# Mean shift of one quarter on VectorE, single PSUM tiles in four places, and one more weight block by seven products

## The chip, the cores and the metric

The kernel runs on one core of a Trainium2 chip. The metric is the device time of one execution in microseconds (us), lower is better. The engines are TensorE (PE in the profile, with its weight loads as PEld), VectorE (DVE), ScalarE (ACT), GpSimd (POOL) and SyncE (SP). SP and POOL issue most of the DMAs.

## The reference

A two-layer decoder trunk for one sequence of 256 tokens and 2048 channels, in float32. Layer 0 mixes tokens by causal pooling over windows of 2, 4, 8 and 16, layer 1 by causal attention with 16 heads of 128 channels, whose keys and values are computed once from the stream after layer 0. Each layer ends with a gated feed-forward network (FFN) that has a causal convolution of width 3.

```python
for i in range(DEPTH):                       # 2
    if i < N_A_LAYERS:                       # layer 0
        mix = pool_mixer(h, pool_w_in[i], pool_w_grp[i], pool_scale[i], pool_w_out[i])
    else:                                    # layer 1
        k_shared = (h @ shared_w_k).reshape(B_, S, N_HEADS, HEAD_DIM)
        v_shared = (h @ shared_w_v).reshape(B_, S, N_HEADS, HEAD_DIM)
        mix = dilated_attention(h, k_shared, v_shared, attn_w_q[j], attn_w_o[j])
    h = layer_norm(DEEPNORM_ALPHA * h + mix, ln1_g[i], ln1_b[i])
    ff = conv_ffn(h, ffn_w_up[i], ffn_conv_w[i], ffn_conv_b[i], ffn_w_down[i])
    h = layer_norm(DEEPNORM_ALPHA * h + ff, ln2_g[i], ln2_b[i])
```

The attention merges three branches of windows (128, 512, 2048) with strides 1, 4 and 16; the branches' softmax denominators weigh them.

## The kernel before

The stream is held transposed, with channels on the partitions, in four quarters of 512 channels: `H[q]` has 128 partitions, 4 channel blocks and 256 tokens. All weights together are read once. The work is a list of units. A unit is one block of weights, mostly 512 by 512 (1 MB): SP loads it to `raw`, ACT casts it to a high part `wh` (L99), DVE subtracts to get the low part `wl` (L100), and PE multiplies. A product in full precision is three: high by high, high by low, low by high (L180 and L181, or L183 to L185). Loads run five units ahead and splits three units ahead. `later(n, f)` puts `f` n units later, `before[i]` puts work ahead of the products of unit i; so each engine's order is fixed by the order in which this code is written out, SP's and POOL's DMA queues too.

For some blocks the 512 by 512 product is made by seven products of half the size in place of eight (Strassen-Winograd). Such a block takes two entries of the list, "a" and "b": DVE forms sums of the weights (L120 to L124), both engines split them (ACT L119 and L113, DVE L121 and L114), and PE does 42 products of 256 columns. Sums of the stream's quarter (`v_sums`, tile `f`, L1001 to L1021) are needed too, and the results are combined in `v_early` and `v_post`.

PSUM is handed out in four pairs of banks. `pair()` gives one pair, `bank()` the first half of one. An instruction that reads or writes a tile waits for the other engines' work on that tile as a whole.

The places of the change, in the order of the span:

- *Start.* `x_quad` (L538 on) transposes a quarter of x by PE (L548) into `xT`, two halves into the two banks of one pair. Per half, ACT casts to `xc` (L553) and DVE subtracts (L554). One unit later ACT copies all 1024 elements to `H` (L557).
- *Mean of the second layer norm of layer 0.* One unit after quarter 0 of the FFN's output is done, `shift` computes the negated partial mean `cs` by a product (L384) and ACT (L389). It is then added to the quarters: DVE for quarter 0 (L394), POOL's accumulate DMA for 1, 2 and 3 (L409). DVE adds the FFN's products (L338, L340) to each quarter, folds sums `S` and sums of squares `Q` (L364 to L370), and PE reduces them over partitions with L429 and L430. Between them the keys of head group 0 begin (tile `xp`).
- *Attention.* The heads are worked in four groups (`hq`) of four. For each group: units for k, q and v, then scores (PE L1064), softmax on DVE (L1067 to L1082) and ACT, a transposition on DVE (L1088, tile `pb`), sixteen small DMAs from SP and POOL to `pTs` (L1101), and the products with v (L1114, L1115, tile `o`), split by L1119 and L1120.
- *End.* `finish1` (L937 on) does the last layer norm for half of the tokens: PE forms bias terms in `gb` (L940, L947), DVE adds them (L952, L955).

Of the kernel before, what the change touches and what calls it, by code (L numbers as in the profile page):

```python
# [32 lines left out]
def trunk(ctx: ExitStack, tc: tile.TileContext, x, pool_w_in, pool_w_grp, pool_scale, pool_w_out,  # L33
# [348 lines left out]
    def shift(s, first, lay, which):  # L382
# [10 lines left out]
        def one():  # L393
            V.tensor_tensor(H[0], H[0], cb, OP.add)  # L394
            if first:
                pre(1)
            stats(0)

# [14 lines left out]
        if not first:  # L413
            for q in (1, 2, 3):
                less(q)
# [120 lines left out]
    def x_quad(q, halves=(0, 1)):  # L536
        xin = XIN
        if halves[0] == 0:  # L538
            H[q] = hp.tile([P, 4, T], F32, name="h", tag="h")
            XC[q] = quad_tile("xc")  # L540
        if halves[0] == 0:
            ST["xT"] = pair("xT")
        both = ST["xT"]
        for half in halves:
            for kk in range(2):
                for t in range(2):
                    k = 2 * half + kk
                    PE.transpose(both[:, half, kk * T + t * P:kk * T + t * P + P], xin[q, t][:, k * P:(k + 1) * P],  # L548
                                 ident)
        for half in halves:  # L550
            pv2 = both[:, half, :].rearrange("p (k t) -> p k t", k=2)
            s = slice(2 * half, 2 * half + 2)
            A.copy(XC[q][:, s, 0, :T], pv2)  # L553
            V.tensor_tensor(XC[q][:, s, 1, :T], pv2, XC[q][:, s, 0, :T].bitcast(F32), OP.subtract)  # L554
        if halves[-1] == 1:
            before.setdefault(min(q + 1, 3), []).append(
                lambda: A.copy(H[q], both.rearrange("p b (k t) -> p (b k) t", k=2)))  # L557

# [305 lines left out]
    def tm_post(lay, n, c):  # L864
# [68 lines left out]
        def finish1():  # L933
# [3 lines left out]
            g, b = [ST["g"][:, cc, :] for cc in range(4)], [ST["b"][:, cc, :] for cc in range(4)]  # L937
            ps = [p[:, i, :] for p in (pair("gb"), pair("gb")) for i in range(2)]
            for cc in range(3):
# [31 lines left out]
    def v_post(c):  # L971
        def post(t, ps):
            v = v_tile(c)[t]
            if c > 0:
                V.tensor_tensor(v, v, ps, OP.add)
            elif t == 0:
                A.copy(v, ps)
            else:
                V.tensor_copy(v, ps)
        return post  # L980
# [14 lines left out]
    def v_sums(q, then):  # L995
        ap = pools["attn"]
        x = H[q]
        a11, a12, a21, a22 = (x[:, k::2, t * P:t * P + P] for k, t in ((0, 0), (1, 0), (0, 1), (1, 1)))
        f = ap.tile([P, 4, T], F32, name="f", tag="k")
        d = [f[:, i].rearrange("p (k t) -> p k t", k=2) for i in range(4)]  # L1000
# [26 lines left out]
    def qk_post(nm, hq):  # L1027
# [3 lines left out]
        def evac(ps):  # L1031
# [11 lines left out]
            if nm == "q":  # L1043
# [7 lines left out]
                if hq == 0:  # L1051
                    later(4, lambda: v_sums(3, lambda: v_sums(1, lambda: v_sums(2, lambda: None))))
        return post
# [51 lines left out]
    def outputs(hq, ms):  # L1105
        if ms[0] == 0:
            oq[hq] = quad_tile("o")
        vt = vts[hq]
        both = pair("o")
        for m in ms:  # L1110
            hd = slice(m * P, (m + 1) * P)
            ps = both[:, m % 2, :]
            t = pT.pop((hq, m))
            PE.matmul(ps[:, :T], vt[:, 0, hd], t[:, :T], start=True, stop=False)  # L1114
            PE.matmul(ps[:, P:T], vt[:, 1, hd], t[:, T:], start=False, stop=True)  # L1115
        o = oq[hq][:, ms[0]:ms[0] + 2]
        for at in (slice(0, 1), slice(1, 2)) if hq == 3 else (slice(0, 2),):
            hi = o[:, at, 0, :T]
            A.copy(hi, both[:, at, :T])  # L1119
            V.tensor_tensor(o[:, at, 1, :T], both[:, at, :T], hi.bitcast(F32), OP.subtract)  # L1120

    def v_group(hq):
        js = (0, 1, 2, 3)
        seven = {0: (), 1: (1, 2, 3), 2: (1, 2, 3), 3: (3,)}[hq]
        group_tm(shared_w_v, rows4, 512 * hq, 512, xsrcs, v_post(hq),
# [152 lines left out]
```

## Time and profile before

| what | us |
|---|---|
| median of 3 runs | 2025.73 (2024.69 to 2026.8) |
| profiled execution, whole | 2024.98 |
| its span in the trace | 2023.2 |
| PE busy | 2011.6 (99%) |
| PE weight loads busy | 1813.7 (90%) |
| DVE busy | 1728.5 (85%) |
| ACT busy | 1269.2 (63%) |
| POOL busy | 94.3 (5%) |
| mean granted TensorE clock | 0.999 of full speed |

A row of the timeline gives the start in us, the duration, the engine, the line, the operation, what it writes and reads, and in brackets how long the engine stood idle before it and what ended that. The list of waits gives, for an engine, the idle time by the instruction that waited and what it waited for: total, times, mean. A row of windows gives the stretch, its length, the busy time of PE, PEld, DVE, ACT and POOL (with the number of instructions), then the granted clock, the DMA engines' busy share and GB/s.

### The profile page before, as it was taken

The numbers are of one execution on the slowest core, as the hardware profiler recorded it, in microseconds if no ns is written. First come the engines' busy times: TensorE is split into PE (matmuls) and PEld (weight loads), VectorE is DVE, ScalarE is ACT, GpSimd is POOL, SyncE is SP. The second block draws the span as 40 slices with busy tenths as digits, with TensorE's granted clock in tenths as the row PEclk, the third lists the DMA queues.
The fourth block names the chain that finished last, engine by engine and source line by source line (L and its number), as shares of the span: only waits on it lengthen the run. The fifth ranks groups of instructions, "written<-read, shape, count | busy, mean of one in ns | idle before, by whom it ended". The sixth has DMA issues, their size and how long they took to land.

```text
span 2023.2 us, 31428 instructions
## 1 busy us (share of the span) xinstructions
PE 2011.6 (99%) x12742; PEld 1813.7 (90%) x12742; DVE 1728.5 (85%) x1822; ACT 1269.2 (63%) x1546; POOL 94.3 (5%) x154
## 2 busy tenths in 40 slices
PE   9999999999999999999999999999999999999999
PEld 8898988999899988888898988998899989989987
DVE  6868887999899999779796878787899899989898
ACT  5454686766766676656554444477767677667672
POOL 2000000000000000000000021000000000000000
PEclk9999999999999999999999999999999999999999
DMA  8565576676666767885565656557666757666765
GB/s 256 192 211 188 164 216 191 180 221 222 197 198 205 233 190 219 236 226 187 177 207 165 199 175 207 188 175 221 167 215 203 227 179 227 193 222 189 211 220 173
DMA packets 271825, 408.30 MB, mean 202 GB/s; under 512 B 74446, under 2 KB 86116, under 8 KB 271424
## 3 DMA queue, kind: packets, MB, share of 16 engines
q1 hardware_dynamic: 259488, 388.93, 59.1%
q0 software_dynamic: 11760, 16.70, 5.5%
q8 instruction: 100, 1.64, 0.3%
q10 hardware_dynamic: 432, 0.66, 0.1%
q14 instruction: 45, 0.37, 0.1%
HBM read 380.01 MB, written 2.10 MB: 189 GB/s over the span
## 4 chain that ended last, share of the span: by engine, by line
PE 98%; DVE 1%; DMA 0%; issue 0%; ACT 0%; SPq 0%; DVEq 0%
PE acc L180 44%; PE acc L181 22%; PE s L246 3%; PE s L244 3%; PE s L245 3%; PE acc L185 3%; PE t L246 2%; PE t L244 2%; PE t L245 2%; PE acc L184 2%; PE acc L183 2%; PE t L255 2%; PE t L257 2%; PE t L256 2%; PE s L1064 0%; PE o L1114 0%
## 5 line engine op out<-in xcount | busy, mean ns | idle before, releaser
L180 PE MATMUL acc<-xc,wh 128*128 128x512 f32 x3264 | 1151.8, 396 | 0.0
L181 PE MATMUL acc<-xc,wl 128*128 128x256 f32 x3264 | 916.0, 281 | 0.0
L100 DVE TENSOR_TENSOR wl<-raw,wh 128x2048 fp32r<-128x2048 f32 (+2 forms) x305 | 657.1, 2163 | 174.9 <-ACT wh L99 170.3
L180 PEld LDWEIGHTS acc<-xc,wh 128*128 128x128 f32 x3264 | 616.0, 189 | 143.3
L99 ACT CAST wh<-raw 128x2048 fp32r<-128x2048 f32 (+2 forms) x305 | 548.7, 1805 | 170.1 <-PE acc L180 70.4
L181 PEld LDWEIGHTS acc<-xc,wl 128*128 128x128 f32 x3264 | 615.4, 189 | 0.1
L113 ACT CAST wh<-raw 128x1024 fp32r<-128x1024 f32 x142 | 148.4, 1052 | 194.5 <-DVE raw L122 175.3
L114 DVE TENSOR_TENSOR wl<-raw,wh 128x1024 fp32r<-128x1024 f32 x142 | 169.4, 1221 | 11.2 <-ACT wh L113 11.2
L121 DVE TENSOR_TENSOR wl<-raw,wh 128x1536 fp32r<-128x1536 f32 x71 | 124.5, 1754 | 6.7 <-ACT wh L119 5.7
L119 ACT CAST wh<-raw 128x1536 fp32r<-128x1536 f32 x71 | 104.9, 1477 | 35.4 <-PE acc L180 28.2
L287 POOL DMA_DIRECT2D ht<-w x48 | 41.3, 1014 | 1446.7 <-DVE ht L877 722.1
L246 PE MATMUL t<-wh,g 128*128 128x256 f32 x376 | 105.7, 281 | 0.0
L244 PE MATMUL t<-wh,g 128*128 128x256 f32 x376 | 105.6, 281 | 0.0
L245 PE MATMUL t<-wl,g 128*128 128x256 f32 x376 | 105.4, 280 | 0.0
L620 ACT ACTIVATE c<-u,cv 128x256 f32<-128x256 f32 x172 | 89.5, 592 | 23.1 <-DVE f L682 16.6
L246 PE MATMUL s<-wh,xs 128*128 128x256 f32 x344 | 96.2, 280 | 0.0
L244 PE MATMUL s<-wh,xs 128*128 128x256 f32 x344 | 96.1, 279 | 0.0
L245 PE MATMUL s<-wl,xs 128*128 128x256 f32 x344 | 96.0, 279 | 0.0
L124 DVE TENSOR_TENSOR raw<-raw 128x1024 f32<-128x1024 f32 x71 | 87.0, 1225 | 2.4
L625 ACT ACTIVATE a<-u,cv 128x256 f32<-128x256 f32 x172 | 73.4, 499 | 11.9 <-DVE g L692 11.9
L611 ACT COPY u<-acc 128x512 f32<-128x512 f32 x84 | 46.9, 573 | 47.4 <-PE acc L181 47.1
L625 ACT ACTIVATE u<-u,cv 128x256 f32<-128x256 f32 x172 | 73.4, 499 | 0.0
(337 smaller groups left out, 3445.2 us busy)
## 6 DMA issues: line engine op xcount, KB each, us to landing
raw<-in_ffn_w_up_dram SPq DMA_DIRECT2D x160, 1024.0 KB, 5.2
raw<-in_ffn_w_down_dram SPq DMA_DIRECT2D x80, 1024.0 KB, 5.2
raw<-in_pool_w_out_dram SPq DMA_DIRECT2D x16, 1024.0 KB, 5.0
raw<-in_shared_w_k_dram SPq DMA_DIRECT2D x16, 1024.0 KB, 5.1
raw<-in_attn_w_q_dram SPq DMA_DIRECT2D x16, 1024.0 KB, 5.1
raw<-in_shared_w_v_dram SPq DMA_DIRECT2D x16, 1024.0 KB, 5.2
raw<-in_attn_w_o_dram SPq DMA_DIRECT2D x16, 1024.0 KB, 5.4
ht<-w POOLq DMA_DIRECT2D x50, 256.0 KB, 5.3
```

What stands on the lines that cost most here:

```text
L99: A.copy(wh[i][:, s], r[:, s])
L100: V.tensor_tensor(wl[i][:, s], r[:, s], wh[i][:, s].bitcast(F32), OP.subtract)
L113: A.copy(h[:, :, n], r[:, :, n])
L114: V.tensor_tensor(l[:, :, n], r[:, :, n], h[:, :, n].bitcast(F32), OP.subtract)
L119: A.copy(hs, rs)
L121: V.tensor_tensor(ls, rs, hs.bitcast(F32), OP.subtract)
L180: PE.matmul(ps[m].ap, h[:, k, c], q[:, k, :, :T], start=st, stop=False)
L181: PE.matmul(ps[m][:, :T], l[:, k, c], q[:, k, 0, :T], start=False, stop=sp)
L244: PE.matmul(to, xh, h[:, k, n], start=opens and kk == 0, stop=False)
L245: PE.matmul(to, xh, l[:, k, n], start=False, stop=False)
L246: PE.matmul(to, xl, h[:, k, n], start=False, stop=ends and kk == 1)
L625: A.activation(to[:, m, :], u[:, m, i:i + T], AF.Copy, scale=cv[:, i, j:j + 1])
```

## The change

Five things are changed.

1. In the second layer norm of layer 0 DVE adds the mean to quarter 1 as well; POOL's accumulate DMA does so only for quarters 2 and 3.
2. In `x_quad` each half has its own PSUM tile. The copy to `H` is made in two parts of 512 elements, ahead of the products of unit q rather than q + 1.
3. In `finish1` the three products of `gb` have a tile each in place of two pairs.
4. In `outputs`, the second half of the last head group has one tile per head, and each is evacuated right behind its products. The first half of that group is evacuated by one instruction on each engine, as the other groups are.
5. Head group 0 does the block of quarter 3 of v by seven products. The sums of that quarter are formed as soon as q of group 0 is evacuated, in a buffer of the `h` pool; those of quarters 1 and 2 follow six units later. Since the list then has one more entry in this group, the second `blocks` and both `outputs` of the group come one block of weights sooner.

```diff
@@ shift, one
             V.tensor_tensor(H[0], H[0], cb, OP.add)
             if first:
                 pre(1)
+            else:
+                V.tensor_tensor(H[1], H[1], cb, OP.add)
             stats(0)
@@
         if not first:
-            for q in (1, 2, 3):
+            for q in (2, 3):
                 less(q)
@@ x_quad
-        if halves[0] == 0:
-            ST["xT"] = pair("xT")
-        both = ST["xT"]
         for half in halves:
+            ps = bank("xT")
             for kk in range(2):
                 for t in range(2):
                     k = 2 * half + kk
-                    PE.transpose(both[:, half, kk * T + t * P:kk * T + t * P + P], xin[q, t][:, k * P:(k + 1) * P],
-                                 ident)
-        for half in halves:
-            pv2 = both[:, half, :].rearrange("p (k t) -> p k t", k=2)
+                    PE.transpose(ps[:, kk * T + t * P:kk * T + t * P + P], xin[q, t][:, k * P:(k + 1) * P], ident)
+            pv2 = ps.rearrange("p (k t) -> p k t", k=2)
             s = slice(2 * half, 2 * half + 2)
             A.copy(XC[q][:, s, 0, :T], pv2)
             V.tensor_tensor(XC[q][:, s, 1, :T], pv2, XC[q][:, s, 0, :T].bitcast(F32), OP.subtract)
-        if halves[-1] == 1:
-            before.setdefault(min(q + 1, 3), []).append(
-                lambda: A.copy(H[q], both.rearrange("p b (k t) -> p (b k) t", k=2)))
+            before.setdefault(q, []).append(lambda s=s, pv2=pv2: A.copy(H[q][:, s, :], pv2))
@@ finish1
-            ps = [p[:, i, :] for p in (pair("gb"), pair("gb")) for i in range(2)]
+            ps = [bank("gb") for cc in range(3)]
@@ v_post
-            if c > 0:
-                V.tensor_tensor(v, v, ps, OP.add)
-            elif t == 0:
-                A.copy(v, ps)
-            else:
-                V.tensor_copy(v, ps)
+            V.tensor_tensor(v, v, ps, OP.add)
@@ v_sums
-        f = ap.tile([P, 4, T], F32, name="f", tag="k")
+        f = hp.tile([P, 4, T], F32, name="f", tag="h") if q == 3 else ap.tile([P, 4, T], F32, name="f", tag="k")
@@ qk_post
                 if hq == 0:
-                    later(4, lambda: v_sums(3, lambda: v_sums(1, lambda: v_sums(2, lambda: None))))
+                    v_sums(3, lambda: None)
+                    later(6, lambda: v_sums(1, lambda: v_sums(2, lambda: None)))
@@ outputs
-        both = pair("o")
+        last = hq == 3 and ms[0] == 2
+        both = None if last else pair("o")
         for m in ms:
             hd = slice(m * P, (m + 1) * P)
-            ps = both[:, m % 2, :]
+            ps = bank("o") if last else both[:, m % 2, :]
...
+            if last:
+                hi = oq[hq][:, m, 0, :T]
+                A.copy(hi, ps[:, :T])
+                V.tensor_tensor(oq[hq][:, m, 1, :T], ps[:, :T], hi.bitcast(F32), OP.subtract)
-        o = oq[hq][:, ms[0]:ms[0] + 2]
-        for at in (slice(0, 1), slice(1, 2)) if hq == 3 else (slice(0, 2),):
-            hi = o[:, at, 0, :T]
-            A.copy(hi, both[:, at, :T])
-            V.tensor_tensor(o[:, at, 1, :T], both[:, at, :T], hi.bitcast(F32), OP.subtract)
+        if not last:
+            o = oq[hq][:, ms[0]:ms[0] + 2]
+            A.copy(o[:, :, 0, :T], both[:, :, :T])
+            V.tensor_tensor(o[:, :, 1, :T], both[:, :, :T], o[:, :, 0, :T].bitcast(F32), OP.subtract)
@@ v_group
-        seven = {0: (), 1: (1, 2, 3), 2: (1, 2, 3), 3: (3,)}[hq]
+        seven = {0: (3,), 1: (1, 2, 3), 2: (1, 2, 3), 3: (3,)}[hq]
```

ScalarE's order at the start, before the change (`xT` are transposed halves, `raw` and `wh` the weights of the first units):

```order
7 L553 CAST xc<-xT 128x2x256 x2
8 L99 CAST wh_256<-raw_115 128x512 x4
9 L557 COPY h<-xT 128x1024
10 L553 CAST xc<-xT 128x2x256 x2
11 L99 CAST wh_332<-raw_124 128x512 x4
12 L557 COPY h<-xT 128x1024
```

And after it:

```order
7 L553 COPY h<-xT 128x512 x2
8 L551 CAST xc<-xT 128x2x256 x2
9 L99 CAST wh_260<-raw_115 128x512 x4
10 L553 COPY h<-xT 128x512 x2
11 L551 CAST xc<-xT 128x2x256 x2
12 L99 CAST wh_338<-raw_124 128x512 x4
```

The copy of a quarter is in two parts and now stands before the next quarter's casts even for the first quarter; the casts and the weights keep their order.

VectorE's order at the mean, before (`h` is a quarter of the stream, `cs` the negated mean, `fold` a scratch tile):

```order
655 L394 TENSOR_TENSOR h<-h,cs 128x1024
656 L364 TENSOR_TENSOR fold<-h 128x512
657 L367 TENSOR_TENSOR S<-fold 128x256
658 L364 TENSOR_TENSOR fold<-sq 128x512
659 L367 TENSOR_TENSOR Q<-fold 128x256
660 L338 TENSOR_TENSOR h<-h,acc 128x512
```

And after:

```order
655 L394 TENSOR_TENSOR h<-h,cs 128x1024
656 L398 TENSOR_TENSOR h<-h,cs 128x1024
657 L364 TENSOR_TENSOR fold<-h 128x512
658 L367 TENSOR_TENSOR S<-fold 128x256
659 L364 TENSOR_TENSOR fold<-sq 128x512
660 L367 TENSOR_TENSOR Q<-fold 128x256
661 L338 TENSOR_TENSOR h<-h,acc 128x512
```

One addition of 1024 elements stands ahead of the folds of quarter 0; the rest follows as before.

VectorE's order in the attention from q of head group 0 to its first scores (`p<-s`), before:

```order
724 L1042 TENSOR_TENSOR q<-q,acc 128x512 x2
725 L100 TENSOR_TENSOR wl_9294<-raw_9210,wh_9293 128x2048
726 L100 TENSOR_TENSOR wl_9325<-raw_9248,wh_9324 128x2048
727 L1067 SCALAR_TENSOR_TENSOR p<-s,negm 128x768
728 L1070 TENSOR_REDUCE mx<-p 128x2 x2
```

And after:

```order
725 L1033 TENSOR_TENSOR q<-q,acc 128x512 x2
726 L992 TENSOR_TENSOR f<-h 128x256
727 L993 TENSOR_TENSOR f<-f,h 128x256
728 L994 TENSOR_TENSOR f<-h 128x256
729 L995 TENSOR_TENSOR f<-h,f 128x256
730 L120 TENSOR_TENSOR raw_9218<-raw_9218 128x2x256
731 L121 TENSOR_TENSOR wl_9305<-raw_9218,wh_9304 128x2x768
732 L122 TENSOR_TENSOR raw_9218<-raw_9218 128x2x256
733 L124 TENSOR_TENSOR raw_9218<-raw_9218 128x4x256
734 L1012 TENSOR_TENSOR vs_9337<-f,vs_9337 128x256
735 L1012 TENSOR_TENSOR vs_9338<-f,vs_9338 128x256
736 L1012 TENSOR_TENSOR vsQ<-f,vsS 128x256
```

The sums of quarter 3 of the stream and the weight sums of the new seven-product block stand between q and the scores. The low part of that block's other half follows them and then the scores; of the two ordinary subtracts that stood here, the first was this block's own and is replaced by these steps, and the second comes after the scores' first softmax.

## The prediction

> **What bounds the kernel now.** I read the page first, then the list of what TensorE waits for, then the timeline at each of these places.
>
> ```profile
> span 2023.2 us, 31428 instructions
> PE 2011.6 (99%) x12742; PEld 1813.7 (90%) x12742; DVE 1728.5 (85%) x1822; ACT 1269.2 (63%) x1546; POOL 94.3 (5%) x154
> PE 98%; DVE 1%; DMA 0%; issue 0%; ACT 0%; SPq 0%; DVEq 0%
> ...
> PE acc L429 <- DVE S L370: 2.6, 1, 2.6
> ...
> PE acc L185 <- DVE wl L100: 0.9, 3, 0.3
> PE acc L430 <- DVE Q L370: 0.8, 1, 0.8
> ...
> PE acc L180 <- DVE o L1120: 0.5, 2, 0.2
> ```
>
> TensorE (PE) is busy for all but 11.6 us, so only three things can pay: a PE wait that goes, fewer PE columns, or a faster PE clock. The waits (us, times, mean) are small and each has a place. VectorE (DVE), busy 85%, is what PE waits for in every row shown; it can turn from helper into bound locally.
>
> The profiled execution took 2024.98 us, 1.78 more than its span and 0.75 under the median 2025.73. The sum below is made against 2024.98 and then put on the median by adding 0.75. From no change this kernel can be told only beyond about 0.2%, 4.05 us.
>
> **1. Mean shift of quarter 1 on VectorE.** Start, duration, engine, line; at the end the idle time and what ended it:
>
> ```profile
> 893.01 1.22 DVE L394 TENSOR_TENSOR h<-h,cs 128x1024 f32<-128x1024 f32 x1
> 896.32 0.43 DVE L367 TENSOR_TENSOR Q<-fold 128x256 f32<-128x256 f32 x1
> 901.48 0.69 DVE L338 TENSOR_TENSOR h<-h,acc 128x512 f32<-128x512 f32 x1 [4.73 <-DMA h<-cs]
> ...
> 930.28 1.28 DVE L338 TENSOR_TENSOR h<-h,acc 128x512 f32<-128x512 f32 x2
> 934.30 0.43 DVE L370 TENSOR_TENSOR Q<-Q,fold 128x256 f32<-128x256 f32 x1
> ...
> 924.73 0.28 PE L183 MATMUL acc<-xp,wh 128*128 128x258 f32 x1
> 930.38 0.28 PE L185 MATMUL acc<-xp,wl 128*128 128x258 f32 x1
> 933.27 0.70 PE L429 MATMUL acc<-S,onesd 128*128 128x256 f32 x2 [2.61 <-DVE S L370]
> 934.78 1.22 PE L430 MATMUL acc<-Q,onesd 128*128 128x256 f32 x2 [0.82 <-DVE Q L370]
> ...
> 904.96 1.49 ACT L99 CAST wh<-raw 128x1536 fp32r<-128x1536 f32 x1 [3.72 <-PE acc L180]
> 911.55 1.91 ACT L99 CAST wh<-raw 128x2048 fp32r<-128x2048 f32 x1 [4.05 <-DMA raw<-in_shared_w_k_dram]
> ```
>
> DVE idles 4.73 us for the accumulate DMA of quarter 1 and after 901.48 works without a gap until S and Q are done: that delay is what PE pays for 30 us later. The change puts one more instruction like the 1.22 us one ahead of the folds and drops one of three accumulate DMAs on POOL's queue; those of quarters 2 and 3 move up by one place and are needed 10 us later, so I cost them at nothing. The chain Q ends at 896.75 + 1.22 = 897.97, and L338 starts there and not at 901.48: 3.5 us sooner. I walked the row of DVE instructions on from there: each ScalarE input is there in time (the cast of 904.96 ends at 906.45 and its subtract would come at about 906.6; that of 911.55 ends at 913.46, needed at about 914.0), and the last quarter's products end about 924.9, needed at about 926.8. S is then ready at about 929.7, before PE gets there (930.5), and Q at about 931.2: of 2.61 + 0.82 = 3.43 us some 0.2 to 0.3 stay. Waits gained: 3.2.
>
> The wait has a second price, in the windows (busy PE, PEld, DVE, ACT, POOL, then granted clock):
>
> ```profile
> 934.00:934.80 0.80, 0.01 (x1) 0.02 (x1) 0.77 (x3) 0.80 (x1) 0.00 (x0) 1.00 0.95 366
> 934.80:935.40 0.60, 0.60 (x2) 0.51 (x3) 0.60 (x2) 0.60 (x1) 0.00 (x0) 0.50 0.04 14
> ...
> 938.00:938.40 0.40, 0.40 (x4) 0.40 (x4) 0.40 (x1) 0.00 (x0) 0.00 (x0) 0.74 0.00 0
> ```
>
> The granted clock is 0.50 from 934.8 to about 938.2, right after PE was idle for most of 930.5 to 934.6. Half speed for 3.4 us costs 1.7 us of work. If only 0.3 us of idle are left, I see no reason for the drop, and this is gained too. Together 3.2 + 1.7 = 4.9. Bounds: at most 3.43 + 1.7 = 5.1; at least −1.2, if the DMA's end was no true cause and the add is only one more 1.22 us on a busy engine. I take the upper part because every row between was walked.
>
> The Trainium skill, "TensorE: Matmul & The Clock Gate", Part 1, says that the clock gate falls to half rate after at least one idle window of about 3.4 us and rises again after such a window of work. The return after 3.4 us agrees; the fall differs, since here 2.61 us and 0.82 us with 0.7 us of products between them were enough. By the page's word alone the drop would not belong to this wait and the sum would be 1.7 lower, 6.1; the rows decide.
>
> **2. Two transposed tiles at the start.**
>
> ```profile
> 14.01 0.59 ACT L553 CAST xc<-xT 128x512 fp32r<-128x512 f32 x1 [0.76 <-DVE xc L554]
> 14.62 0.69 DVE L554 TENSOR_TENSOR xc<-xT,xc 128x512 fp32r<-128x512 f32 x1 [0.65 <-ACT xc L553]
> 15.97 0.39 PE L185 MATMUL acc<-xc,wl 128*128 128x256 f32 x1 [0.29 <-DVE wl L100]
> 16.57 1.01 ACT L557 COPY h<-xT 128x1024 f32<-128x1024 f32 x1
> 30.29 0.39 PE L185 MATMUL acc<-xc,wl 128*128 128x256 f32 x1 [0.35 <-DVE wl L100]
> 42.05 1.91 ACT L99 CAST wh<-raw 128x2048 fp32r<-128x2048 f32 x1 [4.70 <-DMA raw<-in_pool_w_in_dram]
> ```
>
> With both halves in one pair the two engines take turns: cast, subtract, cast, subtract. With a tile each, ScalarE goes on to the second cast while VectorE subtracts the first, and wl comes some 1.2 us sooner (0.76 less on ScalarE, 0.65 on VectorE), more than the waits it ends. The three waits sum to 0.9 in the list, and each product behind one is 0.11 longer than the 0.28 of a product that waits for nothing: 1.2. In the last quarter three more products run as late behind their subtracts (some 0.13 each by their spacing): 1.6, which I take, with 1.8 as the upper end and 0 as the other, since the load behind the cast at 42.05 was waited for 4.70 us and could swallow it. The copy to H goes from one of 1.01 to two of about 0.57 and moves up ahead of the next quarter's casts, where ScalarE idles over 2 us; the transposes now wait for it, done about 0.5 us sooner than they need it.
>
> **3. One tile per head for the last outputs.**
>
> ```profile
> 1235.66 0.50 PE L180 MATMUL acc<-o,wh 128*128 128x512 f32 x1 [0.23 <-DVE o L1120]
> 1236.52 0.50 PE L180 MATMUL acc<-o,wh 128*128 128x512 f32 x1 [0.24 <-DVE o L1120]
> ```
>
> The first head is evacuated while PE does the second's products, and the second's cast waits no more for the subtract. The two waits of 0.23 and 0.24, each with the 0.11 by which its product is longer than the 0.39 of an ordinary one, make 0.7, which I take; between 0 and 0.8. The other half of that head group, now evacuated in one piece, is needed a unit later and costs nothing.
>
> **4. Three tiles in the last layer norm.**
>
> ```profile
> 2015.57 2.84 PE L947 MATMUL gb<-g,dg 128*128 128x512 f32 x6
> 2017.59 1.41 DVE L952 SCALAR_TENSOR_TENSOR ht<-ht,mv,gb 128x512 f32<-128x512 f32 x2 [0.63 <-PE gb L947]
> ```
>
> DVE's first add waits for both products of a pair; with a tile each only for its own. Then the third product ends at 2018.41 and limits the last piece: 0.4 of 0.63, between 0 and 0.63.
>
> **5. Seven products for the last v unit, with its sums sooner.**
>
> ```profile
> L114 DVE TENSOR_TENSOR wl<-raw,wh 128x1024 fp32r<-128x1024 f32 x142 | 169.4, 1221 | 11.2 <-ACT wh L113 11.2
> L121 DVE TENSOR_TENSOR wl<-raw,wh 128x1536 fp32r<-128x1536 f32 x71 | 124.5, 1754 | 6.7 <-ACT wh L119 5.7
> ...
> 984.45 2.29 DVE L100 TENSOR_TENSOR wl<-raw,wh 128x2048 fp32r<-128x2048 f32 x1 [1.98 <-ACT wh L99]
> 989.37 0.96 DVE L1067 SCALAR_TENSOR_TENSOR p<-s,negm 128x768 f32<-128x768 f32 x1 [2.63 <-PE s L1064]
> 995.88 0.58 PE L255 MATMUL t<-wh,xc 128*128 128x512 f32 x1
> 1001.65 0.39 PE L180 MATMUL acc<-xc,wh 128*128 128x512 f32 x1
> 1042.21 4.60 DVE L100 TENSOR_TENSOR wl<-raw,wh 128x2048 fp32r<-128x2048 f32 x2
> 1047.29 0.39 PE L180 MATMUL acc<-xc,wh 128*128 128x512 f32 x1
> ...
> 989.00:1042.00 53.00, 53.00 (x308) 46.57 (x307) 50.51 (x81) 28.57 (x33) 9.11 (x16) 1.00 0.52 151
> ```
>
> An ordinary v unit takes PE 1001.65 − 995.88 = 5.77 us; 42 products of 256 columns at 0.12 us (5.65 us from 924.73 to 930.38, 47 steps) take 5.04. Gain 0.7, if nothing is late. DVE pays for it: 1.75 + 2 × 1.22, one more step of 1024 elements (1.22) and two of 512 (0.69 each, as L554) replace one 2.29: 4.5 more, some 0.2 less by the overlap of starts. The evacuation grows from one copy of 512 elements to two adds of 256 (0.43 each) and three of 512: about 2.1 more. Some 6.4 are added. The quarter's own sums (eight steps of 256 elements, about 3.2) only move, from after the scores to before them. The idle time before the scores takes 1.98 + 2.63 = 4.6. The rest, 1.8, and some 0.7 in which the second block's transposition waits for the transposed moves, go on as a debt of about 2.5, for from 989 to 1042 DVE is busy 50.51 of 53 us (the third number of the last row). Outputs come a unit sooner, and the eight SP moves now stand ahead of a weight load; the loads are five units ahead, which hides that. The debt reaches PE in the next head group's first q unit: its wl was done at 1044.5 and would be at 1047.0, with PE there at about 1046.5. So 0.5 of 0.7 is lost, net 0.2, between −1.5 (two more units late by half a microsecond or so and this one by 1) and 0.7.
>
> **Sum.** 4.9 + 1.6 + 0.7 + 0.4 + 0.2 = 7.8 us: 2024.98 − 7.8 = 2017.2, on the median 2017.9, 0.39% faster.
>
> **Rivals.**
> - *The wait is shortened, not removed.* If one step of my walk (a cast, a load of w_k) is late by 2 us, S comes after 930.5, about 1.7 us of waits stay, and the half clock with them. Part 1 then brings about 1.5, the total 4.4: 2021.3. For it: ScalarE waits 3.72 us for PE and 4.05 us for a load in this stretch; against: both end before DVE needs them.
> - *The mean does not pay.* The add itself delays the chain and another late input (the DMA of quarter 2, last matrix products) takes the removed wait's place. Parts 2 to 5 remain: 2.9, 2022.8, not to be told from before. Against: L338's products were done about 894.
> - *Slower: DVE's debt in the attention stage.* Place: 989 to 1047, where DVE has 2.5 us free in 53. If the 4.6 us of idle can't be used, because the raw weights or the scores come when they came before, the whole 6.4 us turns into PE waits; add the second transposition held by moves for up to about 5 us (POOL's busy 9.11 us in that window are two rounds of eight such moves, 4.6 each), and one more fall of the clock (1.7): 13.1 us. Then 2024.98 − 7.6 + 13.1 = 2030.5, on the median 2031.2. It decides from a loss of 11.7 us on, 7.6 + 4.05. Against: the seven products are used in later head groups with the same engines and the list shows no such wait there.
> - *The change does not do what it says* in the start: single tiles but the load at 42.05 sets the pace. That costs 1.6 and gives 2019.5, inside the first range.
> - *The clock falls anyway*, because another stretch of idle than that wait sets it off. Then 1.7 of part 1 stay lost: 6.1 gained, 2019.6. Against: over the span the clock averages 0.999, which this one fall of 1.7 in 2023 us already explains, and PE has no other wait over 1.1 us. I count it among the forecast's variants.
>
> **Chances.** Forecast, with its small variants, 0.70 (own range 2016.0 to 2020.0); shortened wait 0.14; mean without effect 0.10; slower 0.06. Faster by over 0.2% (under 2021.7): 0.70 and over half of the shortened wait, 0.79; within 0.2%: the rest of it and the mean without effect, less a little, 0.15; slower 0.06. The range begins at 2016.0, about all upper bounds (5.1 + 1.8 + 0.8 + 0.6 + 0.7 = 9.0, from 2025.73 2016.7) and some scatter, and ends at 2022.5, so that it takes in the shortened wait and leaves out half of the mean without effect and the slower case.
>
> **What would show it.** In the changed profile L429 should have no wait, L430 under 0.5, the granted clock 1.00 around 930 to 936, and L338 should follow Q without a DMA. The three waits at L185 and the two at L180 behind L1120 should be gone, L952's wait be about 0.2. A new wait of PE for wl, of about 0.5, should stand at the first q unit of the second head group. I am wrong if PE waits over 1 us anywhere after 985, or if the clock still falls near 932.

## The result

The changed kernel takes 2016.68 us (median of 6 runs, 2015.05 to 2018.46) against 2025.97 us for the kernel before in the same rounds (6 runs, 2024.69 to 2026.8). The ratio is 0.9955, with a 95% interval of 0.9942 to 0.9968. In later rounds, in the run called `e10_after_again` below, it was 0.9969 (0.9958 to 0.9981), 2016.49 us against 2022.69. So the change is worth 6 to 9 us; the forecast was 7.8. The changed kernel took the same time both times; it is the kernel before that differs, and the experiments show how it varies from one execution to the next.

First the list of what PE waits for in the changed kernel (us in total, times, longest; the third number of the lists ahead of the change is the longest wait too, not the mean, and no term of the prediction hangs on it):

```profile
PE acc L183 <- ACT wh L99: 1.6, 1, 1.6
PE warm L1159 <- DVE one L1155: 1.1, 1, 1.1
PE acc L181 <- DVE wl L100: 0.8, 1, 0.8
PE xT L548 <- DMA xin<-in_x_dram: 0.7, 1, 0.7
PE gb L943 <- DVE dg L941: 0.4, 1, 0.4
PE acc L185 <- DVE wl L100: 0.2, 1, 0.2
```

The waits for S and Q are gone, of the three at the start one of 0.2 is left, and the two behind the last outputs are gone. There are new ones: 1.6 us at the start for a cast, 0.8 us for `wl` and 0.4 us for `dg`. The 1.1 us for `one` at the very start are in both kernels.

The timeline at the mean, where L398 is the added instruction, and the windows behind it (the granted clock is the third number from the end):

```profile
891.14 1.22 DVE L394 TENSOR_TENSOR h<-h,cs 128x1024 f32<-128x1024 f32 x1
892.27 1.22 DVE L398 TENSOR_TENSOR h<-h,cs 128x1024 f32<-128x1024 f32 x1
895.80 0.68 DVE L338 TENSOR_TENSOR h<-h,acc 128x512 f32<-128x512 f32 x1
...
928.63 0.60 PE L431 MATMUL acc<-S,onesd 128*128 128x256 f32 x2
929.29 0.70 PE L432 MATMUL acc<-Q,onesd 128*128 128x256 f32 x2
```

```profile
928.00:932.00 4.00, 3.94 (x29) 3.49 (x28) 3.93 (x8) 3.79 (x5) 0.00 (x0) 1.00 0.35 134
932.00:936.00 4.00, 4.00 (x36) 4.00 (x35) 3.39 (x4) 2.30 (x2) 0.00 (x0) 1.00 0.41 113
```

L338 follows the folds with no wait, S is there when PE comes, and the clock stays at 1.00.

To see where the time went I took the start of each PE product in the changed trace less the start of the same product in the trace of before. A step in this offset is time won or lost at that place; a flat stretch is a stretch in which nothing changed. The same was done for the experiments, always against the first trace of before. The columns below are worked out in this way, in us:

| product of before, by its start | changed | e1 mean only | e2 no mean | e3 no seven | e4 kept busy |
|---|---|---|---|---|---|
| 12.38, behind the second transposes | +0.36 | +1.08 | +0.66 | +0.42 | +0.13 |
| 930.38, last before L429 | −1.87 | +1.20 | −1.61 | −1.79 | +0.13 |
| 938.17, behind the mean | −7.02 | −3.92 | −4.43 | −6.92 | −0.85 |
| 965 to 968, before the attention | −6.74 | −3.64 | −4.14 | −6.63 | −0.85 |
| 1052, second head group | −6.21 | −3.64 | −3.64 | −6.63 | −0.85 |
| 1236.52, behind the last outputs | −7.10 | −3.64 | −4.53 | −7.48 | −0.88 |
| 1990.6, last FFN | −8.22 | −3.64 | −5.65 | −7.48 | −0.88 |
| 2015.57, products with `dg` | −7.69 | −3.63 | −4.97 | −7.49 | −0.88 |
| end of the span | −8.3 | −3.7 | −5.5 | −8.2 | −0.9 |

For the changed kernel: the mean 5.1, the transposes 2.2 (from +0.36 to −1.87), the last outputs 0.89, and from `dg` to the end 0.6. The attention loses 0.5. Two more steps belong to no place that I had named: −1.1 spread over w_o and the second FFN, and +0.5 just ahead of `dg`.

### The profile page after: what moved, and what is told of

It reads as the page before. It is cut to its first block, busy times and chain, and to the rows that moved or that the text cites. A ratio compares the mean times of both kernels' runs of the same rounds, so it can differ in the third digit from the quotient of the medians.

```text
span 2014.9 us, 31474 instructions
## 1 busy us (share of the span) xinstructions
PE 2005.8 (100%) x12760; PEld 1810.2 (90%) x12760; DVE 1734.9 (86%) x1831; ACT 1269.7 (63%) x1551; POOL 93.0 (5%) x153
## 4 chain that ended last, share of the span: by engine, by line
PE 88%; DVE 7%; ACT 2%; DMA 2%; issue 1%; SPq 0%; DVEq 0%; ACTq 0%
PE acc L180 41%; PE acc L181 21%; PE s L244 3%; PE s L246 3%; PE s L245 3%; PE acc L184 2%; PE acc L185 2%; PE acc L183 2%; PE t L246 2%; PE t L244 2%; PE t L245 2%; DVE wl L100 2%; ACT wh L99 1%; DVE wl L114 1%; DVE wl L121 1%
## 5 line engine op out<-in xcount | busy, mean ns | idle before, releaser
L113 ACT CAST wh<-raw 128x1024 fp32r<-128x1024 f32 x144 | 150.7, 1052 | 202.8 <-DVE raw L122 175.5
```

Of the source, the lines that this page charges most:

```text
L113: A.copy(h[:, :, n], r[:, :, n])
```

## Experiments

### The mean alone, and all but the mean

`e1_mean_only` is the kernel before with this, and `e2_no_mean` the changed kernel without it:

```diff
             if first:
                 pre(1)
+            else:
+                V.tensor_tensor(H[1], H[1], cb, OP.add)
...
-            for q in (1, 2, 3):
+            for q in (2, 3):
```

> The kernel before with part 1 alone: VectorE adds the mean to quarter 1, the accumulate DMA does quarters 2 and 3. My theory (the wait of 2.61 + 0.82 us and the half clock behind it go together): about 5 us faster than before, some 2021, the trace the same as that of before up to about 928 and 5 us ahead of it from 932 on, granted clock 1.00 throughout. Rival (the parts need each other, as when the 3.5 us won on VectorE are used up elsewhere): the trace is less than 2 us ahead after 932, or loses part of it by 1050, and the time stays within 2 us of before.

> The changed kernel with part 1 undone (the DMA adds the mean to quarters 1, 2 and 3 again). My theory: 5 us slower than the changed kernel, about 2021.7, with waits of about 2.6 and 0.8 us at the reductions of S and Q and the granted clock at 0.50 for 3.4 us behind them. Rival (the sums of the mean came sooner through another part, the start for instance): under 2 us slower and no fall of the clock.

Measured: e1 2020.33 us, ratio to before 0.9981 (0.9972 to 0.9989), before 2024.7. Its trace makes the step of 5.1 us at the mean, like the changed kernel's, and keeps it through the attention: the theory holds and the parts don't need each other.

e2 2019.45 us, ratio 0.9973 (0.9964 to 0.9983). Neither expectation is met in full: without the mean on VectorE the step is 2.8 us and not 0, so undoing it costs 2.3 us in these two traces. The list of waits, the timeline and the windows of e2:

```profile
PE acc L429 <- DVE S L370: 1.3, 1, 1.3
...
PE acc L430 <- DVE Q L370: 0.8, 1, 0.8
```

```profile
898.58 0.69 DVE L338 TENSOR_TENSOR h<-h,acc 128x512 f32<-128x512 f32 x1 [3.44 <-DMA h<-cs]
```

```profile
932.00:936.00 4.00, 4.00 (x32) 3.95 (x33) 3.94 (x6) 2.40 (x4) 0.00 (x0) 1.00 0.00 2
936.00:940.00 4.00, 4.00 (x36) 4.00 (x35) 3.42 (x4) 2.28 (x2) 0.00 (x0) 1.00 0.83 256
```

VectorE's wait for the accumulate DMA is 3.44 us here and 4.73 in the trace of before, PE's wait for S 1.3 and not 2.6, and the clock does not fall. The DMA landed sooner: L338, which waits for it, starts 9.96 us after POOL's first issue (888.62), in the trace of before 11.25 us after it (890.23). What the mean on VectorE removes is thus a wait whose length differs from run to run.

### The kernel before once more

`e7_before_again` has no edit.

> The kernel before once more, for one look. Theory (the wait for S depends on when the accumulate DMA of quarter 1 lands, and this differs from run to run, 9.9 to 11.3 us after its issue so far; the clock falls only if the wait is long): with a landing near 9.9 us the wait for S is 1.2 to 1.4 us and the clock stays at 1.00, with one near 11.2 us it is 2.6 us and the clock falls to 0.50. Rival (the landing is the same in every run of this kernel): landing 11.2 us, wait 2.6 us, clock 0.50 again.

Measured, in one profiled execution: 2026.5 us. The waits, the timeline and the window:

```profile
PE acc L429 <- DVE S L370: 2.9, 1, 2.9
...
PE acc L430 <- DVE Q L370: 0.8, 1, 0.8
```

```profile
902.95 0.69 DVE L338 TENSOR_TENSOR h<-h,acc 128x512 f32<-128x512 f32 x1 [5.01 <-DMA h<-cs]
```

```profile
936.00:940.00 4.00, 3.76 (x17) 3.58 (x17) 4.00 (x7) 2.84 (x3) 0.00 (x0) 0.57 0.06 22
```

L338 starts 11.53 us after the issue, the wait is 2.9, the clock falls. So of three traces in which PE waits behind this DMA, the two in which L338 starts over 11 us after the issue have the long wait and the fall, and the one with 9.96 has neither. That fits the theory of e7, though a trace of the kernel before itself, unedited and with an early landing, is missing.

It also fits the spread: the kernel before ran between 2021.2 and 2028.0 us over all rounds of these experiments, e1 between 2019.7 and 2021.4. The mean granted clock of every execution is on record as well. Of 78 executions of the kernel before, 24 have a mean of 1.000 and took 2021.2 to 2023.6 us, 39 have 0.999 (2021.7 to 2026.3) and 15 have 0.998 or less (2024.8 to 2028.0); one stretch of 3.41 us at half clock is 0.0008 of such a mean. So in about a third of its executions the kernel before runs without any fall, and it is quicker then. The means do not tell whether a fall lay at the mean shift or at the start, where e7 has one too.

### Work in the wait

`e4_keep` is the kernel before with products that keep PE busy in the wait and that nobody reads:

```diff
+    KEEP = 20
...
     def chain(ps, lay, which, after):
+        if lay == 0 and which == 1:
+            keep = bank("keep")
+            for i in range(KEEP):
+                PE.matmul(keep[:, :P], ident, ident, start=True, stop=True)
```

> The kernel before with 20 products of 128 columns that nobody reads, in the wait ahead of the reductions of S and Q after the first FFN (about 2 us of work in a wait of 2.6). It takes away the idle time and not the wait. My theory (the clock falls because PE is idle there): S and Q come as late as before, the granted clock stays 1.00, and the trace is 1.7 us ahead of before from 940 on: about 2024. Rival (the clock falls for another reason, or the 1.7 us are not a loss): the clock still falls to 0.50 near 934, and the time is that of before.

Measured: 2024.48 us, ratio 1.0003 (0.9994 to 1.0012). The expected time of 2024 is met and says nothing, since before ran at 2024.7 there. The trace tells more:

```profile
930.64 4.63 PE L433 MATMUL keep<-ident 128*128 128x128 f32 x40
935.10 0.60 PE L434 MATMUL acc<-S,onesd 128*128 128x256 f32 x2
935.54 0.59 PE L435 MATMUL acc<-Q,onesd 128*128 128x256 f32 x2
```

```profile
932.00:936.00 4.00, 4.00 (x35) 3.90 (x34) 3.93 (x9) 2.61 (x4) 0.00 (x0) 1.00 0.47 180
936.00:940.00 4.00, 4.00 (x35) 4.00 (x34) 3.33 (x3) 3.80 (x4) 0.00 (x0) 1.00 0.31 86
```

The products took 4.6 us and not 2, so the reduction of Q starts later than before: at 935.54, and 0.63 later when the +0.13 of the start is taken off. Yet the products behind it are 0.98 ahead (from +0.13 to −0.85). The clock stayed at 1.00, and that is worth 0.98 + 0.63 = 1.6 us. So my 1.7 stands as the price of the fall.

That PE's idleness brought the fall is not shown by this run, for S and Q did not come as late as in the trace of before. The DMA landed early here, 10.0 us after its issue at 890.37:

```profile
900.37 0.69 DVE L339 TENSOR_TENSOR h<-h,acc 128x512 f32<-128x512 f32 x1 [3.50 <-DMA h<-cs]
```

S was ready at 932.1, so without the added products PE would have waited about 1.3 us for it, and with that wait the clock of e2 did not fall either.

What speaks for idleness is the record of the clock itself. In all 14 traces the times between two changes of the granted clock are whole multiples of 3.413 us: in the trace of before it is 271 of them from the rise at 9.78 to the fall at 934.79, and one from there to the next rise. So the changes lie on a grid that does not start with the wait. The two windows of the grid around the fall, in the trace of before:

```profile
931.38:934.78 3.40, 0.70 (x2) 0.30 (x2) 3.23 (x8) 3.40 (x8) 0.00 (x0) 1.00 0.92 308
934.80:938.20 3.40, 3.40 (x14) 3.22 (x15) 3.40 (x5) 2.59 (x3) 0.00 (x0) 0.50 0.01 2
```

PE was busy for 0.70 us of the window that ended with the fall, and for 0.70 us of that in e7 too. In e2 the two windows over the wait hold 2.01 and 2.69 us of work. Where the grid lies differs from run to run, so whether a wait of 2.6 us always brings the fall is not shown.

### Without the seven products

`e3_no_seven` is the changed kernel with part 5 undone:

```diff
-            V.tensor_tensor(v, v, ps, OP.add)
+            if c > 0:
+                V.tensor_tensor(v, v, ps, OP.add)
+            elif t == 0:
+                A.copy(v, ps)
+            else:
+                V.tensor_copy(v, ps)
...
-        f = hp.tile([P, 4, T], F32, name="f", tag="h") if q == 3 else ap.tile([P, 4, T], F32, name="f", tag="k")
+        f = ap.tile([P, 4, T], F32, name="f", tag="k")
...
-                    v_sums(3, lambda: None)
-                    later(6, lambda: v_sums(1, lambda: v_sums(2, lambda: None)))
+                    later(4, lambda: v_sums(3, lambda: v_sums(1, lambda: v_sums(2, lambda: None))))
...
-        seven = {0: (3,), 1: (1, 2, 3), 2: (1, 2, 3), 3: (3,)}[hq]
+        seven = {0: (), 1: (1, 2, 3), 2: (1, 2, 3), 3: (3,)}[hq]
```

> The changed kernel with part 5 undone (the first head group's last v unit in the ordinary way, its sums where they were). If part 5 pays 0.2 us as predicted, this is 0.2 us slower than the changed kernel. Rival, from the new wait of 0.84 us of the matrix products for wl at 1041: part 5 costs 0.3 to 0.8 us, and this kernel is that much faster than the changed one; the trace then has no wait of PE between 940 and 1060 and stays about 7 us ahead of before through that stretch.

Measured: 2016.84 us, ratio 0.9962 (0.995 to 0.9975), not to be told from the changed kernel. In the stretch itself the rival is right. The offsets of the changed kernel go from −6.74 to −7.41 at 1037, so the shorter unit gains the 0.7 us that I counted; then the wait comes, and the offset is −6.21 behind it. Here e3 stays at −6.63 with no wait. The rows of the changed kernel:

```profile
1039.95 0.40 PE L180 MATMUL acc<-xc,wh 128*128 128x512 f32 x1
1041.19 0.38 PE L181 MATMUL acc<-xc,wl 128*128 128x256 f32 x1 [0.84 <-DVE wl L100]
...
1034.76 2.23 ACT L113 CAST wh<-raw 128x1024 fp32r<-128x1024 f32 x2 [3.10 <-DVE raw L122]
1036.90 3.71 ACT L99 CAST wh<-raw 128x2048 fp32r<-128x2048 f32 x2
...
1038.84 4.49 DVE L100 TENSOR_TENSOR wl<-raw,wh 128x2048 fp32r<-128x2048 f32 x2 [0.59 <-ACT wh L99]
```

The stall is 1.1 to 1.2 us in all, as the offsets show. The block's `wl` is done at about 1041.1. In before it was done at 1044.5, which less the lead of 6.74 with which the attention began is 1037.8: the debt is 3.3 us. ScalarE is no help, since it waits 3.10 us for VectorE's weight sums (L122) before it comes to this block's cast.

The trace of e3 shows which item of the debt I had wrong. From the evacuation of q of head group 0 to the start of this block's `wl`, VectorE is busy 62.53 us in the changed kernel and 56.42 in e3: 6.1 more, about the 6.4 that I had added up. But of the 4.6 us of idle time ahead of the scores that I set against them, counted in the trace of before, e3 has only 1.55 + 1.85 = 3.4:

```profile
978.60 2.29 DVE L100 TENSOR_TENSOR wl<-raw,wh 128x2048 fp32r<-128x2048 f32 x1 [1.55 <-ACT wh L99]
982.75 0.96 DVE L1063 SCALAR_TENSOR_TENSOR p<-s,negm 128x768 f32<-128x768 f32 x1 [1.85 <-PE s L1060]
```

The other parts had used up the rest: in the changed kernel PE comes to the attention 6.7 us ahead of before and VectorE to q of this group only 5.5 (973.49 for 978.98), so VectorE has 1.2 us less to wait. With the 0.59 us for which it now waits for ScalarE at this block, 6.1 − 3.4 + 0.59 gives the 3.3; directly against e3 this `wl` starts 3.0 us later (1038.84 for 1035.86).

What makes the times equal lies elsewhere. In w_o and the second FFN the changed kernel gains 1.1 us on before, e2 does the same, and e3 and e1 nothing. There is no wait in it. From the start of a product of 512 columns to that of the next product it takes 233.3 to 233.5 ns on the mean in before, e1 and e3, and 232.7 to 232.8 in the changed kernel and e2 (some 1300 such steps that the traces show one by one between 1330 and 1960): 0.6 to 0.8 us of the 1.1, the rest is spread over other products. It repeats to the nanosecond: over that stretch the offset moves by −0.897 us in each of the five traces with part 5 (e5, e6 and e10 below among them) and by 0.000 in the eight others. At the end half of it is lost again, since VectorE is busy from 1992 on with one gap of 0.36 us, and `dg` comes when VectorE gets there (PE's wait of 0.4).

### VectorE's sums on GpSimd

If the new wait is VectorE's debt, taking work off VectorE should end it. `e5_pool_sums` is the changed kernel with the sums of quarters 1 and 2 on GpSimd; `e6_pool_both` moves three multiplications ahead of the last layer norm too:

```diff
+        E = V if q == 3 else nc.gpsimd
-        V.tensor_tensor(d[0], a21, a22, OP.add)
+        E.tensor_tensor(d[0], a21, a22, OP.add)
...
-                    V.tensor_tensor(z, z, ST["g"][:, cc, :], OP.mult)
+                    (nc.gpsimd if t else V).tensor_tensor(z, z, ST["g"][:, cc, :], OP.mult)
```

> The changed kernel, with the sums of quarters 1 and 2 for the first head group (eight steps of 256 elements, about 3 us of VectorE) moved to GpSimd. Theory (the wait for wl at 1041 is VectorE's debt from the seven products): the debt shrinks by 3 us, the wait of 0.84 us goes, and the trace is about 1 us further ahead of the changed kernel from 1045 on; at the end VectorE limits, so the time falls by 0.3 to 0.8 us. Rival (the wait comes from ScalarE's cast or the load of w_q, not from VectorE): the wait stays at about 0.8 us and the time is that of the changed kernel.

> As the run before, and the three multiplications of the second half of the tokens by the gain, ahead of the last layer norm (1.85 us of VectorE), on GpSimd too. Theory (over the last 15 us VectorE has no free time and sets the end): the products for the bias terms wait no more for dg (0.39 us in the changed kernel) and the end comes 0.5 to 1 us sooner than in the run before. Rival (the end is set by the last products, or GpSimd slows VectorE): no gain or a loss against the run before.

Measured: e5 2019.24 us, ratio 0.9976 (0.9967 to 0.9986); e6 2019.0, ratio 0.9978 (0.9969 to 0.9987): both slower than the changed kernel, and neither theory nor rival had foreseen it for e5. The rows of e5, on GpSimd and VectorE, and its new waits of PE:

```profile
1007.56 2.54 POOL L993 TENSOR_TENSOR f<-h 128x256 f32<-128x256 f32 x1
1010.17 2.67 POOL L994 TENSOR_TENSOR f<-f,h 128x256 f32<-128x256 f32 x1
1012.81 0.73 POOL L995 TENSOR_TENSOR f<-h 128x256 f32<-128x256 f32 x1
...
1015.34 1.23 DVE L305 TENSOR_TENSOR xsum<-f,xsum 128x1024 fp32r<-128x1024 f32 x1 [2.20 <-ACT xsum L309]
```

```profile
PE o L1108 <- DVE k L1034: 1.5, 1, 1.5
...
PE acc L181 <- DVE wl L100: 0.8, 1, 0.8
PE s L245 <- DVE wl L114: 0.5, 1, 0.5
```

A step that takes VectorE 0.42 us takes GpSimd 0.73 to 2.67. VectorE's next step on the sums stands in its queue and waits for them, through ScalarE's cast of them (L309), 2.20 and 1.11 us, so VectorE has won nothing; the wait for `wl` is as long as before, and through the attention this trace loses 2.9 us (−4.94 to −2.05) where the changed one loses 0.5. Whether a smaller debt would end the wait stays open, since the experiment did not make it smaller.

VectorE is slowed as well. The subtraction ahead of the end, in the changed kernel and, with GpSimd multiplying beside it, in e6:

```profile
1990.28 1.75 DVE L100 TENSOR_TENSOR wl<-raw,wh 128x1536 fp32r<-128x1536 f32 x1
```

```profile
1993.65 2.78 DVE L100 TENSOR_TENSOR wl<-raw,wh 128x1536 fp32r<-128x1536 f32 x1
```

The Trainium skill, "SBUF — State Buffer", "SBUF: two separate sides", says that VectorE with two inputs from SBUF and GpSimd share a port and that one blocks the other for a whole instruction. That VectorE is slower beside GpSimd agrees with the 2.78 for 1.75 us; that it is blocked for a whole instruction these rows do not show. The end still came a little sooner in e6 than in e5: PE's wait for `dg` is 0.2 and not 0.5, and from 1990 on e6 gains 0.3 us, less than the 0.5 to 1 us that I expected (the other 0.2 us between the spans, 2018.7 and 2019.2, are there from the start). Even this is not shown to come from GpSimd, for the changed kernel without an edit has a wait of 0.2 us for `dg` in `e10_after_again` below.

### What makes the second FFN quicker

Part 5 shifts three rings of buffers by one place: the PSUM pairs, the weight buffers and the h buffers. Four runs were meant to put e3 into the changed kernel's places, one ring at a time (`e8_pad`, `e9_shift`, `e12_hshift`) and two together (`e11_pad_shift`):

```diff
@@ e8_pad and e11_pad_shift: outputs
+        if last:
+            PE.matmul(bank("pad")[:, :P], ident, ident, start=True, stop=True)
@@ e9_shift and e11_pad_shift: do_split
+        if i == marks[2] - 12:
+            for nm in ("wh", "wl"):
+                skip = wp.tile([P, 4, 512], F32R, name=f"skip{nm}", tag=nm)
+                V.memset(skip[:, 0, 0:128].bitcast(F32), 0.0)
@@ e12_hshift: do_split
+        if i == marks[2] - 12:
+            V.memset(hp.tile([P, 4, T], F32, name="skiph", tag="h")[:, 0, 0:128], 0.0)
```

> The changed kernel without part 5, and one more PSUM pair taken at the end of the attention by a product that nobody reads. From there on PSUM pairs are handed out in the phase that the changed kernel has (two places on from before, in place of one). Theory (the products of 512 columns in the second FFN are shorter by 0.5 ns in kernels with part 5 because of that phase): spacing of about 232.7 ns where this kernel without the pair had 233.3, some 1 us over the second FFN. Rival (another consequence of part 5, such as the place of the weight buffers): 233.3 ns, no gain.

> The changed kernel without part 5, and with one buffer of each of the two weight rings (wh, wl, four buffers each) skipped a few units into w_o, so that from there on the weight blocks lie in the buffers where the changed kernel has them. Theory (the products of 512 columns are 0.5 ns shorter in the second FFN of kernels with part 5 because of the place of the weight buffers): spacing of about 232.7 ns from there on, the trace gains some 1 us by 1990 on the kernel without the skip, and the time is 0.5 to 1 us under it. Rival (something else that part 5 shifts, such as the ring of the h buffers): the spacing stays at 233.3 ns, no gain.

> The changed kernel without part 5, with both shifts of the earlier runs together: one PSUM pair taken at the end of the attention, and one buffer of each weight ring skipped. Theory (the shorter 512-column products of the changed kernel need PSUM pairs and weight buffers in the changed kernel's phases both at once): spacing of 232.7 ns in the second FFN and a trace that runs away from the kernel without part 5 by 1 us up to 1990. Rival (it is the h ring, or something else): 233.3 ns.

> The changed kernel without part 5, with one buffer of the h ring (five buffers) skipped, so that the stream's quarters and the token-major sums of the second FFN lie in the buffers where the changed kernel has them. Theory (the place of the h buffers makes the difference): spacing of 232.7 ns in the second FFN, some 1 us gained up to 1990. Rival (not the h ring): 233.3 ns, no gain.

Measured: e8 2017.02 us, ratio 0.9972 (0.996 to 0.9983); e9 2016.79, 0.997 (0.996 to 0.998); e11 2017.16, 0.9971 (0.996 to 0.9983); e12 2020.01, 0.9983 (0.9974 to 0.9992), slowed by new waits of PE at the last outputs (2.3 and 0.9 us). In all four the spacing stays at 233.3 to 233.5 ns in the second FFN and the offset is flat from 1237 on. All four theories fall, and the rival of each holds. The cause of the 0.5 ns stays open; that all three rings are needed at once was not tried.

### The changed kernel once more

> The changed kernel once more, on the same chip and in the same rounds as the run without part 5 and shifted buffers. Theory: 0.3% to 0.45% under before, the wait of 0.84 us for wl at the first q unit of the second head group again and the clock at 1.00 at the mean; the start differs by up to 2 us with the landing of the first weights. If the shifted buffers do what the first theory says, the changed kernel is 0.5 us or so slower than that run; by the rival it is equal to it within 0.3 us.

Measured: 2016.49 us, ratio 0.9969 (0.9958 to 0.9981); e9, in the same rounds, 2016.79. The trace has the wait of 0.84 us for `wl` again, the clock at 1.00 at the mean, and nearly the same offsets: a step of −5.1 at the mean, −6.28 behind the attention's stall, −8.28 at 1990. So these steps repeat. Only ahead of `dg` it loses 0.35 us and not 0.5. No run was quicker than the changed kernel by more than the noise.

## Why the prediction was right, and where it was not

The time (2016.68 for 2017.9) and the direction are right, and the large term is right for the reason given, a wait for the accumulate DMA that moves on to PE with a fall of the clock behind it. That the size fits as well is in part luck: the term was priced from one trace, with a late landing and a fall, and the kernel before has these in some of its executions only. By its steps:

- **Mean, 4.9.** Measured 5.1 in all ten traces with this part, at the upper bound. L338 starts 8.47 us after L394 in the trace of before and 4.66 in the changed one, S was in time, and no wait for Q was left. The clock's 1.7 is 1.6 by e4. What I left out: the wait depends on when the DMA lands. With an early landing (e2) only 2.3 us are to be won. The first trace of before had a late one; e1 was 4.4 us faster than before in the medians, and e2 2.6 slower than e3 in the same rounds.
- **Transposes, 1.6.** Mis-sized: 2.2 to 2.3 in the changed trace, e2 and e3 (+0.36 to −1.87, +0.66 to −1.61, +0.42 to −1.79), over my upper end of 1.8. The steps at the three quarters are about 0.56, 0.53 and 1.19: each of the three waits is worth some 0.16 more than the wait and the 0.11 that I added to it, and of the last quarter's further subtracts, for which I had given 0.13 each, two are worth 0.24. The prediction also left out a wait that part 2 ends: PE's 0.5 us for `xc` ahead of the second transposes (`PE xT L548 <- DVE xc L554` in the list of before). It is 0.5 to 1.0 us in the four traces without part 2 and in none of the ten with it. Yet the changed trace is 0.4 us late behind these transposes, because the start has a delay of its own that differs from run to run: the first weights' second piece was late.

```profile
9.27 1.98 ACT L99 CAST wh<-raw 128x512 fp32r<-128x512 f32 x3 [1.76 <-DMA raw<-in_pool_w_in_dram]
9.94 0.39 PE L183 MATMUL acc<-xc,wh 128*128 128x256 f32 x1 [1.63 <-ACT wh L99]
```

  The trace of before has no such wait of PE, e1 without this part has one of 1.5 and e7, the kernel before itself, one of 1.3: it is not the change's. How long PE waits there says little, since its products of 256 columns ahead of it start 0.21 us apart in the traces of before and e3 and 0.12 apart in the changed one, where the clock rises at 5.38 us and not at about 9.8. So e3 waits only 0.3 for the same late piece and is as late behind it (+0.42). The rival that the load at 42.05 would swallow the gain is refuted, as the offset is flat behind it.
- **Last outputs, 0.7.** 0.89 in the changed trace, 0.85 in e3, a little over my upper end: by spacing the two waits were 0.39 and 0.37 and two more products ran closer together.
- **Last layer norm, 0.4.** From the products with `dg` to the end 0.6 (7.63 to 7.05 us). Not foreseen: PE's gain of the last FFN comes to `dg` before VectorE does, and 0.5 is lost there.
- **Seven products, +0.2.** The sign was wrong at its place. The gain of 0.7 was right; the stall behind it, named for the right block, was 1.1 to 1.2 and not 0.5. The step that failed is the debt "of about 2.5": it was 3.3, against the 2.1 us by which this block's `wl` had been early (2.8 in before, less the 0.7 that PE gained). The item that was too large is the idle time ahead of the scores, 4.6 in before and 3.4 with the other parts in (e3); the added work of 6.4 was 6.1. That part 5 costs no time in all comes from the 0.5 ns per product that I could not have priced and can't explain.

The mis-sized terms nearly cancel: in the changed trace 2.23 + 5.15 + 0.89 + 0.6 − 0.5 from the places, +1.1 and −0.5 from what I didn't know, less 0.4 at the start, and 0.3 of small losses between 938 and 968, give 8.3, the span's difference.

Of the rivals, the shortened wait is what e2 shows for the other kernel: the wait can be 1.3 us without part 1, and then there is less to win. The slower case did not come near: VectorE's idle time ahead of the scores was used, and PE lost 1.2 us at one place, not 13. The clock fell nowhere in the stretch of the mean.

## What to carry to other kernels

When one engine is 99% busy, look up the granted clock in small windows behind each of its waits: here 3.4 us of waiting cost 1.6 us more behind them. A wait on a DMA in the middle of an engine's queue had a price here that differs from run to run; an instruction of 1.2 us on an engine that idled there removed the price and most of the spread. So price such a wait from several executions of the kernel before, not from one. And when one part of a change is to use idle time, count that time with the other parts in place. Last, compare two traces product by product: steps in the offset show at once which parts pay, while the medians of such small parts do not.

## What I had not expected

- An accumulate DMA of 128 by 1024 elements in SBUF took 9.96 to 11.53 us until VectorE could go on. Over 1.6 us of such scatter, one wait of PE went from 1.3 to 2.9 us, and the fall of the clock came or did not.
- The clock fell behind 2.61 + 0.82 us and behind 2.87 + 0.82 us of idle with 0.7 us of work between, not behind 1.30 + 0.82. At the start of e7 it fell behind two waits of 1.3 and 1.0 us, while the changed kernel had one of 1.63 there and no fall. The Trainium skill ("TensorE: Matmul & The Clock Gate", Part 1) has a window of about 3.4 us that runs freely; the grid of 3.413 us on which the clock changes in all traces agrees. PE's work in the window tells these cases apart better than the length of a wait: 0.70 us at the two falls behind the mean, 1.3 to 1.9 at the six falls near the start (e1, e5, e6, e7, e9, e11), but 2.19 and 2.04 in the two windows over which the changed kernel's wait of 1.63 lies. It is not the whole rule, since a window of e12 with 1.56 us of work (1227.68 to 1231.09) has no fall behind it.
- The products of 512 columns took about 232.8 or 233.4 ns to the next product, part of 1.1 us over a stage, depending on something that part 5 moves and that is neither the PSUM pairs' phase, nor the weight buffers', nor both, nor the h buffers', as far as the four runs put these where the changed kernel has them.
